# Gram products of an RWKV scan on halves of the rows, and an SSD branch's decay sums from running sums

## The chip, the cores and the metric

The kernel runs on one core of one Trainium2 chip. The metric is the device time of one execution in microseconds (us). A difference of about 0.2% is what a measurement of this kernel can tell from no change.

The core has five engines, each with its own queue of instructions that it works off in order: TensorE (PE, matrix products; its weight loads stand as PEld in the profile), VectorE (DVE), ScalarE (ACT), GpSimd (POOL) and SyncE (SP, which here issues nearly all the DMAs). An instruction that has to wait holds up all that is queued behind it on its engine.

## What is computed

Two networks run one behind the other on 512 tokens of width 1024, with 256 tokens of context. The first is one block of attention beside a state-space branch (SSD), then a feed-forward layer. The second has four layers: a gated spatial unit (SGU), an RWKV-7 scan, a latent attention (MLA) and a second SGU. The change touches the SSD branch and the RWKV scan. What matters of the SSD reference, for chunks of 128 tokens and 32 heads, forward and backward in time:

```python
cs = jnp.cumsum(ac, axis=-1)                       # running sums of the log decays
cb = jnp.einsum('bclgn,bcsgn->bgcls', cc, bc)
scores = cb[:, :, None] * jnp.exp(segsum(ac))      # segsum: cs[l] - cs[s] for s <= l, else -inf
y_diag = jnp.einsum('bgrcls,bcsgrp->bclgrp', scores, xc)
...
yf, hf = ssd_scan(xf, la[:, :, 0], bm, cm, h0f, with_output)
yb, hb = ssd_scan(jnp.flip(xb, axis=1), jnp.flip(la[:, :, 1], axis=1), ...)
y = yf + jnp.flip(yb, axis=1)
```

The RWKV scan carries a 64x64 state per head through the tokens, in both directions, for 16 heads of 64. The kernel works in chunks of 64 tokens. Within a chunk it needs the products of each head's keys with its receptances and removal vectors, masked by time (the Gram products).

## The kernel before

Every large product is made of three products in a rounded format (high by high, high by low, low by high: lines 101 to 103), with weights loaded by SP into the tile `raw` (line 85, two buffers in the SSD stage), split on ACT or DVE into `whi` and on DVE or POOL into `wlo`, three buffers each. Products of plain fp32 tiles stand in the trace as two records each.

A scheduler in the framework sets the order of the instructions on each engine from a simulated timeline. The code's own order, its generators and its `yield`s (one step of filler work for one step of the scan), and the number of buffers of each tile are what it starts from.

**SSD branch** (`ssd`, from about 505 to 1015 us of the trace; the decays, `ssd_steps`, are made earlier, beside the attention). For each of 4 groups of 8 heads `_ssd_scan` goes over 4 chunks, and in each over 2 half groups `hb` of 4 heads: 32 half groups in all. Beside it run as filler the gate products (`pz`) of the same group and the projections (`px`) of the next, and in the last group the attention's output products (`pa`). A half group builds the sums of log decays between every pair of tokens of the chunk as `pE` (128 x 4 heads x 128): for each direction `d` four multiplications of a mask with one column of `laT` (tile `rr`, on ACT for d = 0, line 1903, on DVE for d = 1, line 1901), then one fp32 product with a second mask (line 1904), the two directions summed in PSUM. ACT takes the exponential into `lx` (line 1908). `dm` (ACT, line 1906, then POOL with `cbs`, line 1909) carries the step sizes and the products of B and C. DVE multiplies the two (line 1910), and four products per half group with `xT` give `pyd` (line 1913). `pE` has two buffers and needs nothing of the group's own data, so its products stand well ahead of their use.

**RWKV scan** (`_rwkv_scan`, about 2780 to 3210 us). Two streams `q` of heads go through 12 segments of 4 chunks, the second two steps behind the first; `chunk` is a chain PE, ACT, PE, ACT and DVE, PE, DVE, and the next chunk's first products need its last result. `prepare` readies a stream's next segment one or two steps ahead, with `yield`s between its parts: loads of `kb` and `ar`, four transposes per direction (`pb`), then for each chunk `i` two fp32 Gram products (`d` = 0, 1; line 992) of 128 rows x 256 columns, and a mask product on DVE (`aq`, line 994). 128 rows hold two heads of 64 (`HR[h]`). `ar[:, i, d, h]` is zero in the other head's rows, so one product over all 128 rows gives both heads side by side. `pgm` has two buffers of one PSUM bank each. Other filler in the scan (`late`) is the triangular inverses, on DVE (`_rwkv_diagonal`) and PE (`_rwkv_inverse`).

Of the kernel before, what the change touches and what calls it, by code (L numbers as in the profile page):

```python
# [18 lines left out]
P = 128  # L19
# [917 lines left out]
def _rwkv_scan(K, pools, psum, psp, W, FE, TD, VT, ZD, O, gam, bon, late):  # L937


    nc = K.nc  # L940
    pool = pools[1]
# [4 lines left out]
    HR = ZR  # L946
# [15 lines left out]
    def prepare(n, q, hp, seg, out):  # L962

        st = slice(seg * 4, seg * 4 + 4)
        ar, zv, td, bk = operands(n, q)
        aqs = []
# [22 lines left out]
        for i in range(4):  # L989
            pgm = psp.tile([P, 2, 2, P], F32, tag="pgm", bufs=2, name=K.nm("pgm"))  # L990
            for d in range(2):
                nc.tensor.matmul(pgm[:, d], kb[:, i, d, :], ar[:, i, d], start=True, stop=True)  # L992
            aqs.append(pool.tile([P, 2, 2, P], F32, tag="aq", bufs=10, name=K.nm("aq")))
            nc.vector.tensor_tensor(aqs[i], pgm, mk, op=ALU.mult)
            if i % 2:
                yield
# [668 lines left out]
def ssd_steps(K, XL, XC, W, keep, tmp, S):  # L1665
# [18 lines left out]
    laT = keep.tile([P, 6, 64], F32, name="laT")  # L1684
    ex = keep.tile([P, 6, 192], F32, name="ex")
    wd = keep.tile([P, 6, 64], F32, name="wd")
    S.update(cw=cw, cb=cb, ng=ng, db=db, mk=mk, dtT=dtT, dd=dd, laT=laT, ex=ex, wd=wd)
# [17 lines left out]
    x = laT  # L1705
# [27 lines left out]
    yield  # L1733
    nc.vector.scalar_tensor_tensor(laT, dtT, -1.0, alog.to_broadcast([P, 6, 64]), op0=ALU.mult, op1=ALU.mult)
# [3 lines left out]
    for j in range(6):  # L1738
        d = j % 2
        pe = K.pm.tile([P, 6, 32], F32, tag="m", name=K.nm("pe"))  # L1740
        nc.tensor.matmul(pe, mk[:, j] if j < 4 else K.ones, laT[:, :, d * 32:d * 32 + 32], start=True, stop=True)
        nc.scalar.activation(ex[:, :, j * 32:j * 32 + 32], pe, AF.Exp)
        yield
    nc.vector.tensor_tensor(wd, dtT, ex[:, :, 64:128], op=ALU.mult)
# [93 lines left out]
def _ssd_scan(K, pool, psum, V, g, A, y):  # L1838

    nc = K.nc  # L1840
    dtT, dd, laT, ex, wd, mk = (V[n] for n in ("dtT", "dd", "laT", "ex", "wd", "mk"))
# [36 lines left out]
    for c in range(4):  # L1878
# [12 lines left out]
        for hb in range(2):  # L1891
            h0 = g * 8 + hb * 4
            dm = pool.tile([P, 4, P], F32, tag="dm", bufs=2, name=K.nm("dm"))

            pE = psum.tile([P, 4, P], F32, tag="e", bufs=2, name=K.nm("pE"))
            for d in range(2):
                rr = pool.tile([P, 4, P], F32, tag=f"rr{d}", bufs=1, name=K.nm("rr"))
                for i in range(4):
                    o = d * 32 + h0 + i
                    if d:  # L1900
                        nc.vector.tensor_scalar(rr[:, i, :], mk[:, d], laT[:, t, o:o + 1], None, op0=ALU.mult)
                    else:
                        nc.scalar.activation(rr[:, i, :], mk[:, d], AF.Copy, scale=laT[:, t, o:o + 1])
                nc.tensor.matmul(pE, mk[:, 2 + d], rr, start=d == 0, stop=d == 1)
            for i in range(4):
                nc.scalar.activation(dm[:, i, :], mk[:, 3], AF.Identity, scale=dd[:, t, h0 + i:h0 + i + 1], bias=dtT[:, t, 32 + h0 + i:33 + h0 + i])
            lx = pool.tile([P, 4, P], F32, tag="lx", bufs=2, name=K.nm("lx"))
# [502 lines left out]
```

## Time and profile before

| | us |
|---|---|
| time, median of 3 runs | 4372.11 (4363.34 to 4372.17) |
| the profiled execution's own time | 4365.29 |
| its span, from the first to the last instruction | 4363.5 |
| granted TensorE clock over the span, share of full speed | 0.952 |
| SSD stage, first to last product of the groups' scans | about 505 to 1015 |
| RWKV scan | about 2780 to 3210 |

The page gives the busy time of each engine over the span, the span in 40 slices, the costliest groups of instructions, and the waits. A line of a group or of a timeline names line, engine, operation, the tile written and the tiles read, the shape, and the number of records. A PE record's duration runs until its results have left the array, so records overlap, and the time that a product takes of PE is the distance to the next start. In a timeline equal neighbours are merged: the second number is then the time from the first start to the last end.

### The profile page before, as it was taken

What the parts mean: (1) busy time and instruction counts of PE and PEld (TensorE: products, weight loads), DVE (VectorE), ACT (ScalarE), POOL (GpSimd) and SP (SyncE); (2) the same over time, 40 slices, a digit from 0 to 9 for tenths busy, and PEclk for the clock granted to TensorE, in tenths of its full rate; (3) what the DMA queues carried; (4) which work ended last, traced back from release to release, by engine and by line L of the source; (5) the groups of instructions that cost most, each with busy time, mean ns of one, the idle gap of its engine ahead of it and who ended that gap; (6) DMA issues with size and microseconds to landing.
All of it is one profiled execution on the core that took longest, in us unless ns stands there. A gap on an engine that the chain in (4) does not pass through costs nothing. (4 is left out here: it accounts for less than half of the span.)

```text
span 4363.5 us, 67568 instructions
## 1 busy us (share of the span) xinstructions
PE 4007.8 (92%) x26396; PEld 3288.7 (75%) x26396; DVE 2739.3 (63%) x4361; ACT 1751.1 (40%) x3331; POOL 1507.5 (35%) x1046
## 2 busy tenths in 40 slices
PE   5888999988989999999988989789989999999999
PEld 3766767656766779888977777577777888888987
DVE  6455476676788884445786687865555466663433
ACT  4445445432233334223343555333323465543321
POOL 4333144443444442222344544534411222211221
PEclk7999999988999999999988998899999999999999
DMA  5113121235444553324534667745512311122222
GB/s 190 60 57 99 54 83 51 85 116 169 145 147 150 168 190 117 97 87 139 174 121 158 222 196 225 188 120 143 139 57 92 102 48 51 53 95 92 90 94 87
DMA packets 345550, 518.45 MB, mean 119 GB/s; under 512 B 114424, under 2 KB 217464, under 8 KB 343696
## 3 DMA queue, kind: packets, MB, share of 16 engines
q1 hardware_dynamic: 339040, 502.08, 37.4%
q10 hardware_dynamic: 6192, 12.06, 0.8%
q8 instruction: 208, 3.41, 0.3%
q14 instruction: 110, 0.90, 0.1%
HBM read 425.86 MB, written 88.19 MB: 118 GB/s over the span
## 5 line engine op out<-in xcount | busy, mean ns | idle before, releaser
L93 POOL TENSOR_TENSOR wlo<-raw,whi 128x1024 fp32r<-128x1024 f32 (+2 forms) x254 | 569.6, 2243 | 1332.8 <-ACT whi L91 960.8
L91 ACT ACTIVATE whi<-raw 128x1024 fp32r<-128x1024 f32 (+3 forms) x399 | 383.4, 962 | 706.4 <-PE pz L102 132.2
L95 DVE TENSOR_TENSOR wlo<-raw,whi 128x1024 fp32r<-128x1024 f32 (+3 forms) x278 | 350.2, 1261 | 288.4 <-ACT whi L91 282.1
L127 DVE SCALAR_TENSOR_TENSOR macc<-mraw,conds,macc 128x1024 f32<-128x1024 f32 x168 | 272.0, 1634 | 36.8 <-DMA mraw<-mw 36.5
L103 PE MATMUL pu<-xh,wlo 128*128 128x512 f32 x608 | 243.0, 400 | 10.3 <-DVE wlo L95 6.5
L102 PE MATMUL pu<-xl,whi 128*128 128x512 f32 x608 | 242.1, 398 | 1.1 <-DVE xl L258 1.1
L101 PE MATMUL pu<-xh,whi 128*128 128x512 f32 x608 | 240.4, 399 | 2.9 <-DVE fu L2063 2.4
L89 DVE CAST whi<-raw 128x1024 fp32r<-128x1024 f32 (+2 forms) x133 | 99.5, 748 | 150.1 <-PE pz L102 46.6
L226 POOL TENSOR_TENSOR rsr<-rsv,mhalf 128x4 f32<-128x4 f32 (+3 forms) x56 | 77.9, 1391 | 276.3 <-DVE rsv L224 258.7
L102 PE MATMUL pz<-xl,whi 128*128 128x512 f32 x384 | 150.0, 391 | 0.0
L101 PE MATMUL pv<-whi,xh 128*128 128x256 f32 x512 | 139.0, 283 | 7.0 <-ACT whi L91 6.2
L103 PEld LDWEIGHTS pu<-xh,wlo 128*128 128x128 f32 x608 | 116.0, 191 | 39.0 <-DVE wlo L95 7.3
L102 PE MATMUL pv<-wlo,xh 128*128 128x256 f32 x512 | 142.1, 282 | 0.0
L103 PE MATMUL pv<-whi,xl 128*128 128x256 f32 x512 | 140.2, 282 | 0.5 <-DVE xl L258 0.5
L101 PEld LDWEIGHTS pu<-xh,whi 128*128 128x128 f32 x608 | 116.1, 191 | 31.8 <-issue 3.5
L102 PEld LDWEIGHTS pu<-xl,whi 128*128 128x128 f32 x608 | 116.0, 191 | 29.1 <-DVE xl L258 1.8
L102 PE MATMUL po<-slo,whi 128*128 128x512 f32 (+1 forms) x384 | 136.1, 357 | 0.0
L103 PE MATMUL po<-shi,wlo 128*128 128x512 f32 (+1 forms) x384 | 135.4, 357 | 0.0
L101 PE MATMUL po<-shi,whi 128*128 128x512 f32 (+1 forms) x384 | 133.9, 364 | 0.5 <-ACT shi L111 0.5
L992 PE MATMUL pgm<-ar,kb 128*128 128x256 f32 x384 | 116.8, 427 | 18.9 <-DMA ar<-fe 15.7
L334 POOL TENSOR_TENSOR u<-u,z 128x512 f32<-128x512 f32 (+1 forms) x48 | 58.5, 1218 | 165.2 <-DVE z L325 165.2
L101 PE MATMUL pl<-xlh,whi 128*128 128x512 f32 x208 | 93.3, 452 | 13.2 <-DVE rp L1488 10.2
(747 smaller groups left out, 12923.8 us busy)
## 6 DMA issues: line engine op xcount, KB each, us to landing
mraw<-mw SPq DMA_DIRECT2D x128, 512.0 KB
raw<-G_wuz SPq DMA_DIRECT2D x96, 512.0 KB
raw<-G_wv SPq DMA_DIRECT2D x48, 512.0 KB
raw<-G_wout SPq DMA_DIRECT2D x48, 512.0 KB
raw<-F_w_up SPq DMA_DIRECT2D x44, 512.0 KB
raw<-R_w_in SPq DMA_DIRECT2D x70, 256.0 KB
raw<-S_w_xbc SPq DMA_DIRECT2D x24, 512.0 KB
fe<-ra SPq DMA_DIRECT2D x16, 768.0 KB
```

The source lines that it names most:

```text
L89: nc.vector.tensor_copy(hi, raw)
L91: nc.scalar.activation(hi, raw, AF.Copy)
L93: nc.gpsimd.tensor_tensor(lo, raw, hi.bitcast(F32), op=ALU.subtract)
L95: nc.vector.tensor_tensor(lo, raw, hi.bitcast(F32), op=ALU.subtract)
L101: nc.tensor.matmul(ps, a[0], b[0], start=start, stop=False)
L102: nc.tensor.matmul(ps, a[0], b[1], start=False, stop=False)
L103: return nc.tensor.matmul(ps, a[1], b[0], start=False, stop=stop)
L127: nc.vector.scalar_tensor_tensor(acc, raw, c[:, kt:kt + 1], acc, op0=ALU.mult, op1=ALU.add)
L226: nc.gpsimd.tensor_tensor(r, v, self.mhalf[:, :n], op=ALU.pow)
L334: nc.gpsimd.tensor_tensor(u, u, z, op=ALU.mult)
L992: nc.tensor.matmul(pgm[:, d], kb[:, i, d, :], ar[:, i, d], start=True, stop=True)
```

## The change

There are two parts, and nothing else is edited.

In the RWKV scan a chunk's two Gram products over 128 rows become four over 64 rows: for each direction and head one of `kb[HR[h]]` with `ar[HR[h], ..., h]`, 128 columns wide, so the zero rows are no longer read. `pgm` becomes one tile of two PSUM banks, one bank for each head, holds two chunks, and has one buffer; the mask product of DVE reads it with its dimensions exchanged.

In the SSD branch the running sums of the log decays, of which `ssd_steps` already made the exponentials (`pe`), are also copied as they are (`cum`), transposed, and written to DRAM as rows (`cumrows`, 4 chunks x 64 x 128). In the scan a half group loads for each direction four rows, each spread over all 128 partitions (`cr`, two DMAs of 256 KB on SP's queue, two buffers). ACT adds the negative running sum of the token on the partition to the forward rows, DVE adds it to the backward rows and takes the smaller of the two, the exponential is taken in place, and the product with `dm` too. `rr`, `pE` and `lx` are gone.

```diff
-        for i in range(4):
-            pgm = psp.tile([P, 2, 2, P], F32, tag="pgm", bufs=2, name=K.nm("pgm"))
-            for d in range(2):
-                nc.tensor.matmul(pgm[:, d], kb[:, i, d, :], ar[:, i, d], start=True, stop=True)
...
-            nc.vector.tensor_tensor(aqs[i], pgm, mk, op=ALU.mult)
-            if i % 2:
-                yield
+        for i0 in (0, 2):
+            pgm = psp.tile([P, 2, 2, 2, P], F32, tag="pgm", bufs=1, name=K.nm("pgm"))
+            for i in range(2):
+                for d in range(2):
+                    for h in range(2):
+                        nc.tensor.matmul(pgm[:, h, i, d], kb[HR[h], i0 + i, d, :], ar[HR[h], i0 + i, d, h], start=True, stop=True)
+            for i in range(2):
...
+                nc.vector.tensor_tensor(aqs[i0 + i], pgm[:, :, i].rearrange("p h d t -> p d h t"), mk, op=ALU.mult)
+            yield
...
+        if j < 2:
+            nc.scalar.activation(cum[:, :, j * 32:j * 32 + 32], pe[:, 2:], AF.Copy)
         yield
+        if j == 1:
+            pr = K.pm.tile([64, 4, P], F32, tag="m", name=K.nm("prow"))
+            for t in range(4):
+                nc.tensor.transpose(pr[:, t, :], cum[:, t, :], K.ident)
+            row = raw[:, 0:4 * P].rearrange("h (c t) -> h c t", t=P)
+            nc.scalar.activation(row, pr, AF.Copy)
+            nc.sync.dma_start(rows.rearrange("c h t -> h c t"), row)
+            nc.vector.tensor_scalar(cum, cum, -1.0, None, op0=ALU.mult)
+            yield
...
-            pE = psum.tile([P, 4, P], F32, tag="e", bufs=2, name=K.nm("pE"))
+            cr = pool.tile([P, 2, 4, P], F32, tag="cr", bufs=2, name=K.nm("cr"))
             for d in range(2):
-                rr = pool.tile([P, 4, P], F32, tag=f"rr{d}", bufs=1, name=K.nm("rr"))
-                for i in range(4):
-                    o = d * 32 + h0 + i
-                    if d:
-                        nc.vector.tensor_scalar(rr[:, i, :], mk[:, d], laT[:, t, o:o + 1], None, op0=ALU.mult)
-                    else:
-                        nc.scalar.activation(rr[:, i, :], mk[:, d], AF.Copy, scale=laT[:, t, o:o + 1])
-                nc.tensor.matmul(pE, mk[:, 2 + d], rr, start=d == 0, stop=d == 1)
+                nc.sync.dma_start(cr[:, d], rows[c:c + 1, d, h0:h0 + 4].to_broadcast([P, 4, P]))
+            for i in range(4):
+                nc.scalar.activation(cr[:, 0, i, :], cr[:, 0, i, :], AF.Identity, bias=cum[:, c, h0 + i:h0 + i + 1])
+                nc.vector.scalar_tensor_tensor(cr[:, 0, i, :], cr[:, 1, i, :], cum[:, c, 32 + h0 + i:33 + h0 + i], cr[:, 0, i, :],
+                                               op0=ALU.add, op1=ALU.min)
...
-            nc.scalar.activation(lx, pE, AF.Exp)
+            lx = cr[:, 0]
+            nc.scalar.activation(lx, lx, AF.Exp)
```

The order of the instructions moves with it. On PE in the SSD stage, in the first group's third chunk, before (`pE_5105` is the first half of the fourth chunk, `pyd_4847` the output product):

```order
L103 MATMUL px_5041<-xlh_198,wlo_5002 128x512
L1904 MATMUL pE_5105<-rr_5106,smk 128x512
L1904 MATMUL pE_5105<-rr_5112,smk 128x512
L1870 MATMUL pof_5079<-S_4835,CF_3981 128x512
L1815 MATMUL pxT_4967<-ident,cu_4960 128x128 x4
L1913 MATMUL pyd_4847<-xTl_3977,lx_4866 128x64 x4
L101 MATMUL px_5140<-xch_168,whi_5136 128x256
```

and now, at the same place:

```order
L1832 MATMUL pxT_4927<-ident,cu_4920 128x128 x2
L1888 MATMUL pof_5072<-S_4834,CF_3992 128x512
L1832 MATMUL pxT_4963<-ident,cu_4956 128x128 x4
L1928 MATMUL pyd_4846<-xTl_3988,cr_4848 128x64 x4
L1875 MATMUL pst_5082<-x_1051_5080,BTl_3990 128x512
L1928 MATMUL pyd_4846<-xTl_3988,cr_4970 128x64 x4
L101 MATMUL px_5130<-xch_168,whi_5126 128x256
```

The `pE` products are gone, and the `pyd` products of both half groups stand close together.

On SP in the same stage, before (`raw` are weight loads, `mraw` loads for a later layer's modulation):

```order
L85 DMA raw_5134<-S_w_xbc 128x1024
L85 DMA raw_5240<-S_w_xbc 128x1024
L85 DMA raw_5343<-S_w_xbc 128x1024
L85 DMA raw_5495<-S_w_z 128x1024
L122 DMA mraw_5131<-mw 128x1024
```

and now:

```order
L85 DMA raw_5227<-S_w_xbc 128x1024
L1915 DMA cr_4654<-cumrows 128x512 x2
L1915 DMA cr_4714<-cumrows 128x512 x2
L85 DMA raw_5330<-S_w_xbc 128x1024
L85 DMA raw_5482<-S_w_z 128x1024
L1915 DMA cr_4848<-cumrows 128x512 x2
L1915 DMA cr_4970<-cumrows 128x512 x2
L122 DMA mraw_5121<-mw 128x1024
```

The four `cr` loads of a chunk stand between the weight loads; with two buffers, those of one chunk wait for the `pyd` products of the chunk before.

On PE in the RWKV scan, before (`c` are the chain's products; two different chunks' Gram products, a set of transposes between them):

```order
L1009 MATMUL c_4671_24238<-S_24193,ar_23999 64x64 x2
L992 MATMUL pgm_24410<-ar_24150,kb_24160 128x256 x2
L985 MATMUL pb_24223<-ident,ks_24222 128x128 x4
L992 MATMUL pgm_24415<-ar_24150,kb_24160 128x256 x2
L1014 MATMUL c_4672_24239<-xs_24248,td_24001 64x64
```

and now:

```order
L1012 MATMUL c_4661_24624<-S_24523,ar_23977 64x64 x2
L995 MATMUL pgm_24879<-ar_23914,kb_24490 128x128 x8
L1010 MATMUL c_4674_24688<-zv_24078,aq_24349 64x64 x2
L1012 MATMUL c_4674_24688<-S_24582,ar_24077 64x64 x2
L1010 MATMUL c_4674_24688<-zv_24078,aq_24349 64x64 x2
```

The eight products of two chunks stand in one row here; over the whole scan the Gram products stand in 93 stretches, 98 before.

## Rows read from the trace of the kernel before

**Rows 1.** The page's head: span; busy us (share) and instructions of each engine.
```profile
span 4363.5 us, 67568 instructions
...
PE 4007.8 (92%) x26396; PEld 3288.7 (75%) x26396; DVE 2739.3 (63%) x4361; ACT 1751.1 (40%) x3331; POOL 1507.5 (35%) x1046
```

**Rows 2.** Busy time by stretch: PE, PEld, DVE, ACT, POOL; PEclk; DMA share; GB/s.
```profile
505.00:930.00 425.00, 407.97 (x1933) 303.89 (x1931) 276.46 (x421) 202.22 (x430) 192.32 (x140) 0.97 0.23 72
930.00:1015.00 85.00, 67.99 (x232) 43.48 (x231) 67.96 (x83) 20.37 (x47) 42.10 (x28) 0.86 0.39 130
2800.00:3163.00 363.00, 330.69 (x5456) 266.27 (x5456) 221.82 (x584) 131.86 (x353) 161.76 (x155) 0.96 0.53 139
```

**Rows 3.** PE's timeline, SSD stage: start, us, engine, line, what, records; idle before.
```profile
607.26 1.02 PE L1904 MATMUL pE<-rr,smk 128*128 128x512 f32 x2
608.12 1.02 PE L1870 MATMUL pof<-S,CF 128*128 128x512 f32 x2
...
610.45 1.10 PE L1913 MATMUL pyd<-xTl,lx 128*128 128x64 f32 x8
```

**Rows 4.** Line L1904 over the whole trace: ns min/median/max, first and last start.
```profile
L1904 PE MATMUL pE<-rr,smk x128: 590/592/1191, 467.6 to 956.0; 128*128 128x512 f32 x128
```

**Rows 5.** DVE's groups, 455 to 1015 us: busy, mean ns, idle before by releaser.
```profile
L1901 DVE TENSOR_SCALAR rr<-smk,laT 128x128 f32<-128x128 f32 x128 | 46.8, 425 | 8.5 <-PE pE L1904 5.8 <-DMA ad<-ao 2.5
...
L1910 DVE TENSOR_TENSOR lx<-lx,dm 128x512 f32<-128x512 f32 x32 | 37.0, 1174 | 0.0
```

**Rows 6.** ACT's groups in the same stretch.
```profile
L1906 ACT ACTIVATE dm<-smk,dtT,dd 128x128 f32<-128x128 f32 x128 | 52.2, 483 | 50.3 <-DVE lx L1910 50.3
L1903 ACT ACTIVATE rr<-smk,laT 128x128 f32<-128x128 f32 x128 | 40.7, 390 | 16.0 <-PE pE L1904 15.7
...
L1908 ACT ACTIVATE lx<-pE 128x512 f32<-128x512 f32 x32 | 18.5, 582 | 3.2 <-PE pyd L1913 3.2
```

**Rows 7.** PE's waits, 455 to 985 us: us in total, times, longest.
```profile
PE pyd L1913 <- DVE lx L1910: 5.8, 4, 1.9
```

**Rows 8.** SP's timeline: one weight load's issue.
```profile
675.89 0.33 SPq L85 DMA_DIRECT2D raw<-S_w_xbc  x1
```

**Rows 9.** DVE's timeline: the first work on that load.
```profile
679.12 0.89 DVE L89 CAST whi<-raw 128x1024 fp32r<-128x1024 f32 x1 [1.19 <-PE pz L102]
```

**Rows 10.** SP's own waits, 455 to 985 us.
```profile
SPq L85 <- DVE wlo L95: 258.0, 26, 27.2
```

**Rows 11.** PE's timeline: the pyd products of first chunks of groups 0, 3.
```profile
555.95 1.22 PE L1913 MATMUL pyd<-xTl,lx 128*128 128x64 f32 x10
...
572.63 1.56 PE L1913 MATMUL pyd<-xTl,lx 128*128 128x64 f32 x13
...
928.36 1.00 PE L1913 MATMUL pyd<-xTl,lx 128*128 128x64 f32 x8
...
945.43 1.78 PE L1913 MATMUL pyd<-xTl,lx 128*128 128x64 f32 x15
```

**Rows 12.** PE's timeline in the RWKV scan.
```profile
2937.38 1.13 PE L992 MATMUL pgm<-ar,kb 128*128 128x256 f32 x4
2938.44 0.45 PE L1014 MATMUL c<-xs,td 128*64 128x64 f32 x8
```

**Rows 13.** Lines L992 and L994 over the whole trace.
```profile
L992 PE MATMUL pgm<-ar,kb x384: 379/379/796, 2787.3 to 3161.8; 128*128 128x256 f32 x192
...
L994 DVE TENSOR_TENSOR aq<-pgm,r_rmask x96: 669/684/693, 2790.7 to 3164.8; 128x512 f32<-128x512 f32 x96
```

**Rows 14.** PE's timeline, RWKV features: products on half the rows and columns.
```profile
2420.28 1.61 PE L793 MATMUL pM<-ra,bk 64*64 64x64 f32 x48
```

**Rows 15.** PE's waits in the scan, 2780 to 3210 us.
```profile
PE pgm L992 <- DMA ar<-fe: 15.7, 9, 5.7
```

**Rows 16.** ACT's timeline, the scan's end: the xs copy, the two streams in turn.
```profile
3167.79 0.28 ACT L1011 ACTIVATE xs<-c 128x128 f32<-128x128 f32 x1 [0.63 <-PE c L1009]
...
3171.44 0.28 ACT L1011 ACTIVATE xs<-c 128x128 f32<-128x128 f32 x1 [0.68 <-PE c L1009]
```

More of the change, by code (lines that the diff above doesn't have):

```diff
@@ L987, in prepare @@
         yield
-        for i in range(4):
-            pgm = psp.tile([P, 2, 2, P], F32, tag="pgm", bufs=2, name=K.nm("pgm"))
-            for d in range(2):
-                nc.tensor.matmul(pgm[:, d], kb[:, i, d, :], ar[:, i, d], start=True, stop=True)
-            aqs.append(pool.tile([P, 2, 2, P], F32, tag="aq", bufs=10, name=K.nm("aq")))
-            nc.vector.tensor_tensor(aqs[i], pgm, mk, op=ALU.mult)
-            if i % 2:
-                yield
+        for i0 in (0, 2):
[5 more added lines that the diff above has]
+            for i in range(2):
+                aqs.append(pool.tile([P, 2, 2, P], F32, tag="aq", bufs=10, name=K.nm("aq")))
+                nc.vector.tensor_tensor(aqs[i0 + i], pgm[:, :, i].rearrange("p h d t -> p d h t"), mk, op=ALU.mult)
+            yield
     def chunk(hp, seg, i, tiles, S, y):
@@ L1683, in ssd_steps @@
     dd = keep.tile([P, 6, 32], F32, name="dd")
-    laT = keep.tile([P, 6, 64], F32, name="laT")
     ex = keep.tile([P, 6, 192], F32, name="ex")
     wd = keep.tile([P, 6, 64], F32, name="wd")
-    S.update(cw=cw, cb=cb, ng=ng, db=db, mk=mk, dtT=dtT, dd=dd, laT=laT, ex=ex, wd=wd)
+    x = keep.tile([P, 6, 64], F32, name="cum")
+    cum = x[:, 0:4]
+    rows = K.dram.tile([4, 64, P], F32, name="cumrows")
+    S.update(cw=cw, cb=cb, ng=ng, db=db, mk=mk, dtT=dtT, dd=dd, ex=ex, wd=wd, cum=cum, rows=rows)
     dbias = tmp([P, 1, 64], "dbias")
@@ L1703, in ssd_steps @@
         nc.tensor.transpose(pt[:, t, :], raw[:, t * P:(t + 1) * P], K.ident[0:64, 0:64])
-    x = laT
     nc.vector.tensor_tensor(x, pt, dbias.to_broadcast([P, 6, 64]), op=ALU.add)
@@ L1733, in ssd_steps @@
     yield
+    laT = s
     nc.vector.scalar_tensor_tensor(laT, dtT, -1.0, alog.to_broadcast([P, 6, 64]), op0=ALU.mult, op1=ALU.mult)
@@ L1840, in _ssd_scan @@
     nc = K.nc
-    dtT, dd, laT, ex, wd, mk = (V[n] for n in ("dtT", "dd", "laT", "ex", "wd", "mk"))
+    dtT, dd, ex, wd, mk, cum = (V[n] for n in ("dtT", "dd", "ex", "wd", "mk", "cum"))
+    rows = V["rows"].rearrange("c (d h) t -> c d h t", d=2)
     xT, BT, BF, CF = A["xT"], A["BT"], A["BF"], A["CF"]
@@ L1893, in _ssd_scan @@
             dm = pool.tile([P, 4, P], F32, tag="dm", bufs=2, name=K.nm("dm"))
-            pE = psum.tile([P, 4, P], F32, tag="e", bufs=2, name=K.nm("pE"))
+            cr = pool.tile([P, 2, 4, P], F32, tag="cr", bufs=2, name=K.nm("cr"))
             for d in range(2):
-                rr = pool.tile([P, 4, P], F32, tag=f"rr{d}", bufs=1, name=K.nm("rr"))
-                for i in range(4):
-                    o = d * 32 + h0 + i
-                    if d:
-                        nc.vector.tensor_scalar(rr[:, i, :], mk[:, d], laT[:, t, o:o + 1], None, op0=ALU.mult)
-                    else:
-                        nc.scalar.activation(rr[:, i, :], mk[:, d], AF.Copy, scale=laT[:, t, o:o + 1])
-                nc.tensor.matmul(pE, mk[:, 2 + d], rr, start=d == 0, stop=d == 1)
+                nc.sync.dma_start(cr[:, d], rows[c:c + 1, d, h0:h0 + 4].to_broadcast([P, 4, P]))
[3 more added lines that the diff above has]
+                                               op0=ALU.add, op1=ALU.min)
             for i in range(4):
                 nc.scalar.activation(dm[:, i, :], mk[:, 3], AF.Identity, scale=dd[:, t, h0 + i:h0 + i + 1], bias=dtT[:, t, 32 + h0 + i:33 + h0 + i])
-            lx = pool.tile([P, 4, P], F32, tag="lx", bufs=2, name=K.nm("lx"))
-            nc.scalar.activation(lx, pE, AF.Exp)
+            lx = cr[:, 0]
+            nc.scalar.activation(lx, lx, AF.Exp)
             nc.gpsimd.tensor_tensor(dm, dm, cbs.rearrange("p (o l) -> p o l", o=1).to_broadcast([P, 4, P]), op=ALU.mult)
```

## The prediction, made before the changed kernel ran

> **What bounds the kernel now.** I read the page's head first: PE is busy for 92% of the span and no other engine for more than 63% [rows 1]. What decides is the stage, so the second view was the busy time by stretch [rows 2]. In the SSD stage from 505 to 930 us PE works 408 of 425 us at a granted clock of 0.97, while DVE, ACT and POOL have half their time or more free: PE work taken out there comes off the time nearly whole, until the next engine or a wait takes over. From 930 to 1015 us PE works 68 of 85 us; waits bind there, and work taken from PE is worth less. In the scan PE is busy for 331 of 363 us, but this is many small products of a chain; DVE has 61% and DMA 53%. So the scan is bound mostly by what PE issues, and in part by the chain and by loads.
>
> The third view was PE's timeline, because a record's duration overlaps the next; only distances between starts are PE time.
>
> **SSD: what goes.** A `pE` product (two records) starts at 607.26, the next product at 608.12: 0.86 us, though its line shows 590 ns a record [rows 3, 4]. There are 128 records, hence 64 products: 64 x 0.86 = 55 us of PE. On DVE 128 `rr` (46.8 us) go and 128 additions with a minimum of the same size come, taken at the same 425 ns: even [rows 5]. On ACT 128 `rr` (390 ns) go and 128 additions of a bias come, which are the form of `dm` (483 ns): 128 x 0.09 = +12 us [rows 6]. ACT is 48% busy there [rows 2], so I take this at nothing. If that cover is gone it costs at most these 12 us.
>
> **SSD: what comes.** 64 loads of 256 KB go to SP's queue, and with them a loop that was not there. `pE` needed no load and stood far ahead. Now `cr` has two buffers, one per half group, so the load for a chunk can start only when the `pyd` of the chunk before has read the buffer. One round of that loop: a load of 512 KB takes 3.2 us from issue to first use [rows 8, 9], which is what the two DMAs of a half group move. Then ACT 4 x 0.48 = 1.9, the last DVE addition 0.4, the exponential 0.6, the DVE product 1.2 [rows 5, 6]; for the second half group ACT needs another 1.9 + 0.6; the `pyd` products take 1.0. Sum 10.8 us. Two chunks' `pyd` blocks stand 16.7 and 17.1 us apart in the first and last group [rows 11]. Less four `pE` of 0.86 this becomes 13.3 to 13.7. So the loop fits, with 2.5 to 3 us to spare, when nothing stands in its queues. Something does stand there: ACT and SP work in order. A bias addition that waits for its load holds up the evictions of `pxT`, the convolution's copies and the weight splits behind it, for which PE then waits. And SP's loads stand behind weight loads. Today `pyd` waits only 4 times, 5.8 us in all, for its DVE operand [rows 7]. For the new wait the bounds are 0 (the spare time holds) and 3 us a chunk (the spare time again, used up twice over), times 16 chunks: 0 to 48. I take 1 us a chunk, nearer to rows 7 than to the upper end, because the filler on PE is large products that need no decay: 16 us. SSD together: -55 + 16 = -39, range -55 to -7.
>
> **The decays beside the attention.** Four transposes, three copies, one store and one more step in a stretch of large products: +2 us, 0 to 4, bounded by a few products of 0.1 to 0.4 us and one chain step.
>
> **Scan: what goes and comes.** The 384 Gram records have 256 columns. By `pE` (512 columns in 0.43 us a record) one costs 0.215 us of PE: 83 us. Their stretch of four records took 1.06 us, 0.2 more than that, which is the entry to another tile shape and back [rows 12]; the stretches' number hardly falls (98 to 93 in the order), so that stays. Each record becomes two, on half the rows and with 128 columns. How long is one? 16 `pyd` records (15 are in the row) last 1.78 us: 0.111 each, with 64 columns, where the columns alone would take 0.054 [rows 11]. Loading 128 columns of weights sets that pace, and 128 moving columns also take 0.11. If the two heads' halves run side by side, a pair costs 0.111: 384 x 0.111 = 43 us, a gain of 40. That they do is read from `pM`, whose products on quarters of the array follow at 1.61/48 = 0.03 us [rows 14]; those differ in rows and columns, the new ones in rows only, so the row is near but not the same.
>
> From a product on all rows I would expect 768 x 0.111 = 85 us, no gain. This is where the Trainium skill speaks against the change: "TensorE: Matmul & The Clock Gate", "LDWEIGHTS (loading the stationary operand)", says that a load's time goes by its columns, whatever its rows, and the change doubles the number of loads. By it, with loads in sequence, the sum would be the second rival's below. The same page's "The mechanism" (Part 3) lets work on different row groups overlap; by that the sum is the forecast's. The `pyd` rows agree with the first, `pM` with the second, and no row shows two loads of 128 columns on two halves of the rows.
>
> How much of the 40 reaches the time? The chain is not the bound: a step of one stream, run almost alone at the end, takes 3.65 us [rows 16], while the 96 steps over 363 us (48 for each of two streams) leave 7.6 us for a step of both streams. But PE also waits there, for `ar` loads alone 15.7 us [rows 15], and a shorter scan with 53% DMA [rows 2] will wait more. The mask product on DVE keeps its 669 to 693 ns [rows 13]; one buffer of two banks in place of two of one lets PE fill only when both chunks' masks are done, 1.4 us of DVE, beside other filler. I take 70%: -28, range -45 (all of it and some entries) to -5.
>
> **Sum.** -39 + 2 - 28 = -65. The profiled execution took 4365.3 us (span 4363.5), 6.8 below the median 4372.1: 4300 against its own time, 4307 against the median.
>
> **Rivals.**
>
> *The halves do not overlap* (the change doesn't do what it says). For it: twice the loads, and PEld is at 266 of 363 us already [rows 2]. Against it: `pM`. The scan gives 0: 4372 - 39 + 2 = 4335. Chance 0.12.
>
> *The new loop eats the SSD's gain.* For it: only two buffers, a loop that fits with under 3 us to spare, and an ACT queue in which a load's wait stops unrelated evictions. Against it: PE's filler. It decides at 55/16 = 3.4 us a chunk: 4372 + 2 - 28 = 4346. Chance 0.15.
>
> *Slower than before: `cr` loads stuck on SP.* SP waits in order for a free `raw` buffer: 26 times, 258 us, 9.9 on average, up to 27.2 [rows 10]. A `cr` load behind such a wait arrives that much later, and with two buffers nothing was loaded ahead. Where this hits 12 of 16 chunks in full, it costs 12 x 9.9 = 119: 4372 - 55 + 119 + 2 - 28 = 4410. It turns into a loss from (55 + 28 - 2)/16 = 5 us a chunk. Against it: in the new order a chunk's four loads stand together, one or two weight loads apart from the next, and part of the waiting is spare time before the load is due. Chance 0.08.
>
> *Better than forecast*: the loop costs nothing and the scan gives all its 40: 4372 - 55 + 2 - 40 = 4279. Chance 0.08.
>
> **How the numbers follow.** The forecast, 4285 to 4335 around 4307, has 0.57. The low end 4272 takes in the better case; the high end 4356 takes in the first two rivals with 10 us for their bounds. Left out are the stuck loads and tails of the others, under 0.2. A measurement of this kernel can tell 0.2%, 9 us. Slower by more: 0.09, the third rival with a tail of the second. Same: 0.07, from the second rival with a weak scan. Faster: 0.84.
>
> **What would show it.** The `pE` line is absent and PE in the SSD stage is shorter by about 55 us: step one. PE's wait of `pyd` for the DVE product, 5.8 us before, stays under 20 us, and the waits for `pxT` and split weights don't grow; `pyd` blocks stand 12 to 15 us apart: step two. If they stand at 17 or more, the loop decided, and SP's own waits or ACT's wait for `cr` name which queue. In the scan an eight-product Gram stretch of a chunk pair lasts about 1.1 us if the halves overlap and 2 us if not; the waits for `ar` tell what was given back. The forecast is wrong if these stretches are not shorter per chunk, or if the granted clock, 0.97 and 0.96 in the two stages, falls because PE waits more.

## The result

The changed kernel is slower: 4391.6 us (4380.8 to 4404.3) against 4366.3, ratio 1.0059 with an interval of 1.0046 to 1.0072. I forecast 4307, 65 us under the 4372.1 that stood ahead of the prediction. Its profiled execution took 4384.5 us, 19.2 more than that of before.

The page's head of the changed kernel, then its busy time by stretch (PE, PEld, DVE, ACT, POOL; PEclk; DMA share; GB/s): the SSD stage's two stretches, and the scan from its first Gram product to the first product behind it.

```profile
span 4382.7 us, 68271 instructions
...
PE 3977.6 (91%) x26656; PEld 3301.2 (75%) x26656; DVE 2749.5 (63%) x4362; ACT 1755.1 (40%) x3334; POOL 1522.4 (35%) x1046
...
505.00:930.00 425.00, 382.23 (x1866) 293.80 (x1864) 295.16 (x443) 210.41 (x449) 210.75 (x147) 0.96 0.38 117
930.00:1015.00 85.00, 61.32 (x208) 42.52 (x206) 54.30 (x74) 22.53 (x44) 32.18 (x21) 0.72 0.36 121
...
2777.00:3192.00 415.00, 355.57 (x6159) 302.26 (x6160) 235.45 (x624) 138.96 (x370) 174.25 (x175) 0.85 0.51 128
```

The scan of the kernel before, cut the same way:

```profile
2787.00:3173.00 386.00, 350.97 (x5784) 282.01 (x5784) 238.02 (x624) 138.11 (x372) 175.62 (x177) 0.95 0.54 138
```

PE is busy 30 us less over the span [rows 1], yet the span is longer. The scan takes 415 us in place of 386, at a granted clock of 0.85 in place of 0.95. That is +29, more than the whole loss. The rest is a gain that shrank. Lines with their first and last start show it: the stage's last gate product (`pz`) and the last product of the branch's projection (`py`), before:

```profile
L103 PE MATMUL pz<-xlh,wlo x128: 389/398/799, 519.9 to 931.9; 128*128 128x512 f32 x128
L103 PE MATMUL py<-ox,wlo x128: 387/389/795, 1057.7 to 1155.7; 128*128 128x512 f32 x128
```

and after:

```profile
L103 PE MATMUL pz<-xlh,wlo x128: 389/399/799, 512.9 to 906.6; 128*128 128x512 f32 x128
L103 PE MATMUL py<-ox,wlo x128: 388/389/793, 1039.3 to 1145.0; 128*128 128x512 f32 x128
```

25 us were gained at the last gate product, and 11 are left 240 us later, about as many as when the scan begins (2776.9, before 2787.3). So the profiled execution is 10 us ahead at the start of the scan and loses 29 in it: +19. These are two single executions; the medians differ by 25 us.

**The halves do overlap.** PE's timeline of the changed kernel, two stretches of eight Gram products (two chunks) and what follows each:

```profile
3001.89 2.08 PE L995 MATMUL pgm<-ar,kb 64*128 64x128 f32 x16
3003.90 0.69 PE L1022 MATMUL c<-zv,bk 128*64 128x64 f32 x8
...
3007.42 1.16 PE L995 MATMUL pgm<-ar,kb 64*128 64x128 f32 x16
3008.51 0.66 PE L1130 MATMUL pt<-ident,y 128*128 128x128 f32 x4
```

and their line over the whole trace (ns min/median/max, first and last start):

```profile
L995 PE MATMUL pgm<-ar,kb x768: 272/272/579, 2776.9 to 3181.2; 64*128 64x128 f32 x192
```

Sixteen records in 1.16 us, of 0.27 us each, start (1.16 - 0.27)/15 = 0.06 us apart, 0.12 a pair where I had 0.111. The stretch takes 1.09 us to the next start, where two chunks took 2 x 1.06 [rows 12]. That is the 1.1 us that the prediction named as the sign of overlap: two heads at once, and two loads of 128 columns did not follow one another. "The mechanism" (Part 3) of the Trainium skill's "TensorE: Matmul & The Clock Gate" lets loads overlap work on other row groups. The trace agrees with it. (Loads in sequence would have given the prediction's first rival, 4335, and not "the second rival's" sum, as is written there.) The earlier stretch, the same work, takes 2.01 us: its granted clock was 0.50, 1.2 GHz.

### The profile page after: what moved, and what is told of

The parts are those of the page before. It is cut to its first block, busy times and chain, and to the rows that moved or that the text cites. A ratio compares the mean times of both kernels' runs of the same rounds, so it can differ in the third digit from the quotient of the medians.

```text
span 4382.7 us, 68271 instructions
## 1 busy us (share of the span) xinstructions
PE 3977.6 (91%) x26656; PEld 3301.2 (75%) x26656; DVE 2749.5 (63%) x4362; ACT 1755.1 (40%) x3334; POOL 1522.4 (35%) x1046
## 5 line engine op out<-in xcount | busy, mean ns | idle before, releaser
L127 DVE SCALAR_TENSOR_TENSOR macc<-mraw,conds,macc 128x1024 f32<-128x1024 f32 x168 | 258.1, 1552 | 21.2 <-DMA mraw<-mw 20.5
L995 PE MATMUL pgm<-ar,kb 64*128 64x128 f32 x768 | 91.2, 334 | 24.3 <-DMA ar<-fe 12.1
L887 DVE TENSOR_TENSOR tm<-lm,lw 128x31 f32<-128x31 f32 (+15 forms) x186 | 93.1, 501 | 19.6 <-DMA lm<-md 13.5
```

Of the source, the lines that this page charges most:

```text
L127: nc.vector.scalar_tensor_tensor(acc, raw, c[:, kt:kt + 1], acc, op0=ALU.mult, op1=ALU.add)
L887: nc.vector.tensor_tensor(tv, lm[:, 0:u, u:u + 1].to_broadcast([P, u, 32 - u]), lw[:, u:u + 1, u:32].to_broadcast([P, u, 32 - u]), op=ALU. ...
L995: nc.tensor.matmul(pgm[:, h, i, d], kb[HR[h], i0 + i, d, :], ar[HR[h], i0 + i, d, h], start=True, stop=True)
```

## Experiments

Times are medians beside runs of the kernel before on the same chip (its median was 4365 to 4370 in each of these groups, so a comparison across groups can be off by some us). "Scan" is always cut as above.

### The two parts apart, and what PE's time in the scan is worth

`gram_only` and `ssd_only` take one part each. `gram_one_head` saves the same 40 us of PE without halves, by leaving out the other head's products:

```diff
-                nc.tensor.matmul(pgm[:, d], kb[:, i, d, :], ar[:, i, d], start=True, stop=True)
+                nc.tensor.matmul(pgm[:, d, 0], kb[:, i, d, :], ar[:, i, d, 0], start=True, stop=True)
```

`pairs_full_rows` has the new tile and steps with the old products:

```diff
-                    for h in range(2):
-                        nc.tensor.matmul(pgm[:, h, i, d], kb[HR[h], i0 + i, d, :], ar[HR[h], i0 + i, d, h], start=True, stop=True)
+                    nc.tensor.matmul(pgm[:, i, d], kb[:, i0 + i, d, :], ar[:, i0 + i, d], start=True, stop=True)
...
```

> The Gram part alone, the SSD branch as before. In the trace of the changed kernel the scan, from its first Gram product to the first product behind it, took 415.3 us in place of 385.8 (+29.5). Theory order (the chain now waits behind filler in PE's queue): the loss belongs to this part, time of before +25 to +32, PE's waits for zv and ks as in the changed kernel. Theory clock (half-row products let the granted clock fall): the same total, and a mean clock in the scan near 0.85. If the loss came from the SSD part in some way, this one would be 20 to 40 us faster than before.

> The SSD part alone, the scan as before. In the changed kernel the last gate product of the SSD stage ended 25.4 us sooner, but by the end of the branch's output projection only 10.7 us were left. Expected: 8 to 14 us faster than before, the scan with its old duration (385 us). If the give-back behind the SSD stage belonged to the changed scan, 25 us faster.

> The kernel before, but each Gram product reads the columns of one head alone (128 in place of 256), over all rows, and the mask product reads that half twice: the other head's products are left out. Buffers, yields and their places as before; PE loses 384 x 0.1 = 40 us of issue, as much as side-by-side halves were to save. Theory order: the scan is not bound by what PE issues, gain 0 to 10 us. Theory clock, with PE's issue as the bound: gain 25 to 35 us, the clock as before, near 0.95.

> The Gram part's tile and steps (two chunks per pgm, one buffer of two banks, one yield behind both) with the old products over all 128 rows and 256 columns. Theory order: the pairs in one buffer do the harm, 15 to 40 us slower than before. Theory clock: within 6 us of before, the clock in the scan near 0.95.

Measured: `gram_only` 4404.7 (1.0090, 1.0064 to 1.0116), `ssd_only` 4378.9 (1.0031, 1.0020 to 1.0043), `gram_one_head` 4339.4 (0.9939, 0.9918 to 0.9961), `pairs_full_rows` 4376.5 (1.0025, 1.0011 to 1.0038). Their scans, in this order:

```profile
2783.00:3209.00 426.00, 358.76 (x6153) 304.93 (x6155) 234.16 (x626) 139.28 (x370) 173.03 (x177) 0.83 0.50 126
```

```profile
2789.00:3185.00 396.00, 355.25 (x5784) 289.68 (x5783) 232.47 (x615) 138.70 (x372) 171.23 (x169) 0.92 0.51 132
```

```profile
2782.00:3148.00 366.00, 315.16 (x5810) 274.82 (x5811) 239.59 (x628) 138.35 (x373) 177.25 (x179) 0.92 0.58 146
```

```profile
2786.00:3187.00 401.00, 352.19 (x5797) 290.94 (x5798) 234.75 (x623) 138.86 (x372) 174.28 (x175) 0.92 0.53 132
```

`gram_one_head` gains 27 us for 40 us of PE: some 70% reach the time, as I had assumed, and the theory that the scan isn't bound by PE falls; but its clock is 0.92 and not the expected 0.95, and its trace has 20 us of the gain in the scan. The Gram part as halves loses 38 us, more than the 25 to 32 that I expected. The pairs alone cost 10 of them, between the two theories, so the halves make some 28 us worse what should be 40 less. And `ssd_only` loses 12 us where I expected a gain of 8 to 14: its scan, in which nothing is edited, takes 396 us. The two parts' losses, 38 and 12, don't add up to the changed kernel's 25: each kernel has an order of its own.

### Half of the rows, and the clock

`one_head_64rows` is `gram_one_head` on the 64 rows that are not zero. `halves_and_full` adds 96 products over all rows ahead of the halves, 83 us more for PE. `four_full_rows` is `gram_only` with every half product over all 128 rows, so PE has 42 us more to issue. `halves_single` has halves, one chunk at a time:

```diff
-                nc.tensor.matmul(pgm[:, d, 0], kb[:, i, d, :], ar[:, i, d, 0], start=True, stop=True)
+                nc.tensor.matmul(pgm[:, d, 0], kb[HR[0], i, d, :], ar[HR[0], i, d, 0], start=True, stop=True)
...
+            for h in range(2):
+                nc.tensor.matmul(pgm[:, h].rearrange("p i d t -> p (i d) t"), kb[:, i0, 0, :], ar[:, i0:i0 + 2, :, 0], start=True, stop=True)
...
-                        nc.tensor.matmul(pgm[:, h, i, d], kb[HR[h], i0 + i, d, :], ar[HR[h], i0 + i, d, h], start=True, stop=True)
+                        nc.tensor.matmul(pgm[:, h, i, d], kb[:, i0 + i, d, :], ar[:, i0 + i, d, h], start=True, stop=True)
```

> One head's Gram products alone, as in the run with 128 of 256 columns (4339 us), but on that head's 64 rows: the zero rows are no longer read, the products, their number, columns, buffers and steps are the same; the other head's products are left out in both. Theory clock (PE working on half its rows lets the granted clock fall): clock in the scan near 0.85 in place of 0.92, 20 to 40 us slower than 4339, 4360 to 4380. Theory order (the halves are well, but the pairs of chunks and the order they bring are not): the same time within 8 us, clock near 0.92.

> The Gram part alone, and ahead of each pair of chunks two more products over all 128 rows and 512 columns into the same tile, overwritten by the halves: 96 products, 192 records of 0.43 us = 83 us more for PE. Theory clock: the added work keeps the clock up (over 0.9 in the scan, 0.83 without), and pays for more than half of itself: under 40 us slower than the Gram part alone (4405). Theory order: 60 to 85 us slower than it, 4465 to 4490, the clock unchanged.

> The Gram part alone, with its pairs of chunks, its tile and its four products of 128 columns per chunk, but each over all 128 rows (the zero rows are read again): PE has the Gram products' old cost of 85 us and not 43. Theory clock: the clock in the scan is back above 0.9, and although PE has 42 us more to issue, the time is no longer than with the halves (4405) and near that of the pairs with 256 columns: 4370 to 4390. Theory order: the halves did save their 40 us and the pairs' order costs more, so this is 30 to 45 us slower than the halves, 4435 to 4450.

> Halves of the rows, but one chunk at a time and the yields as before (a tile of two banks, half filled, one buffer). If the pairs in one buffer are what costs (10 us with full rows), this is 10 us faster than the Gram part alone, 4390 to 4397. If the halves themselves cost by the clock, it stays 25 us or more over the kernel before, with a clock in the scan under 0.88.

Measured: 4361.1 (0.9997, 0.9980 to 1.0015), 4450.7 (1.0197, 1.0182 to 1.0213), 4389.6 (1.0046, 1.0028 to 1.0064) and 4402.8 (1.0083, 1.0059 to 1.0108). Their scans:

```profile
2789.00:3168.00 379.00, 337.18 (x5809) 287.54 (x5809) 238.51 (x628) 138.55 (x373) 178.01 (x179) 0.88 0.56 141
```

```profile
2788.00:3257.00 469.00, 418.16 (x6379) 306.80 (x6381) 236.05 (x622) 138.26 (x372) 172.37 (x175) 0.94 0.44 113
```

```profile
2785.00:3198.00 413.00, 362.54 (x6160) 322.14 (x6159) 232.98 (x625) 139.63 (x370) 173.96 (x177) 0.92 0.51 129
```

```profile
2781.00:3209.00 428.00, 363.61 (x6189) 307.29 (x6191) 239.17 (x626) 138.79 (x373) 174.17 (x178) 0.83 0.49 125
```

The same products with the zero rows left out cost 22 us (4361 against 4339), the clock falls from 0.92 to 0.88. Reading the zero rows again, with 42 us more for PE, makes the Gram part 15 us faster (4390 against 4405), the clock is at 0.92 in place of 0.83. The 83 us of added full products cost 46, the clock is at 0.94; I had set the line at 40, so this one alone would decide nothing. Taking the chunks singly changes nothing (4403, 0.83), so the pairs are not the main harm. Expected clocks were met in all but `one_head_64rows` (0.88 for 0.85). Four kernels whose Gram products are halves alone (the changed one among them), in different orders, stand at 0.83 to 0.88. The fifteen kernels here whose Gram products are all over full rows, most of them with an order of their own, stand at 0.91 to 0.95.

What a low clock costs here is seen in `gram_only` in stretches at one level or the other, the chain's products `c` alone (PE busy and records; PEclk; DMA share; GB/s):

```profile
2936.80:2950.40 13.60, 6.69 (x173) 1.00 0.77 159
2950.40:2964.10 13.70, 6.94 (x105) 0.50 0.26 62
2964.10:3005.10 41.00, 20.50 (x517) 1.00 0.51 130
3005.10:3025.60 20.50, 7.59 (x104) 0.50 0.71 147
3025.60:3046.00 20.40, 9.09 (x226) 1.00 0.39 110
3046.00:3063.10 17.10, 7.45 (x105) 0.50 0.44 101
3063.10:3090.40 27.30, 13.88 (x337) 1.00 0.54 124
```

At 2.4 GHz 1253 records in 102.3 us, 12.2 each us; at 1.2 GHz 314 in 51.3 us, 6.1. The scan runs at half pace there, waits included. What PE did as the clock fell at 3005, from PE's timeline:

```profile
3002.98 0.43 PE L1017 MATMUL c<-xs,td 128*64 128x64 f32 x8
3006.82 1.12 PE L985 MATMUL pb<-ident,ks 128*128 128x128 f32 x4 [3.41 <-POOL ks L983]
```

It stood in front of a transpose whose operand POOL had not finished, with the chain's products queued behind it. This is one fall of twelve in that scan.

If time at 1.2 GHz is worth half, clock times length is the scan's length at 2.4 GHz throughout, an estimate from the rows above, of one execution each: 367 for the kernel before (0.95 x 386), 354 for `gram_only`, 353 for the changed kernel, 355 for `halves_single`, 380 for `four_full_rows`, 337 for `gram_one_head` and 334 for `one_head_64rows`. So the halves do save 13 us at full clock (26 against the same steps on full rows), and the half pace takes 62 to 73 us in place of 19. The last two kernels, 22 us apart in time, are equal by this measure.

### Where the SSD part's gain goes

`ssd_one_load` loads the rows once a group into a constant tile. `ssd_act_queue` issues the loads from ACT, and `ssd_split` also puts the two directions into tiles of their own. `pe_one_direction` is the kernel before without the second `pE` product, so its sums lack one direction:

```diff
-                nc.sync.dma_start(cr[:, d], rows[c:c + 1, d, h0:h0 + 4].to_broadcast([P, 4, P]))
+                nc.scalar.dma_start(cr[:, d], rows[c:c + 1, d, h0:h0 + 4].to_broadcast([P, 4, P]))
...
-            cr = pool.tile([P, 2, 4, P], F32, tag="cr", bufs=2, name=K.nm("cr"))
+            cf = pool.tile([P, 4, P], F32, tag="cf", bufs=3, name=K.nm("cf"))
+            cb = pool.tile([P, 4, P], F32, tag="cb", bufs=2, name=K.nm("cb"))
...
-                nc.tensor.matmul(pE, mk[:, 2 + d], rr, start=d == 0, stop=d == 1)
+                if d == 0:
+                    nc.tensor.matmul(pE, mk[:, 2 + d], rr, start=True, stop=True)
```

> The SSD part alone, but the rows are loaded once for each group and not for each half group, so the sums are wrong for all but the first half group (the exponential takes a thousandth of them); all operations of ACT, DVE, POOL and PE stay, and the result goes to a tile of its own with two buffers. The scan's order on PE is the same as in the run of the SSD part. Theory loop (loads and their two buffers eat the gain): the last gate product of the SSD stage comes 10 to 20 us sooner than in the SSD part alone, and the time is 4360 to 4370 in place of 4379. Theory DVE (slower operations and another order, not the loads): within 5 us of 4379. The scan, which has the same order, should have the length of the SSD part's, 396 us.

> The SSD part alone, its 64 row loads issued by ACT and not by SP. If the wait behind weight loads on SP is the loop's price: the SSD stage 10 us shorter. If the loop is slow by its own steps: no change in the stage. The scan's order on PE is closer to that of the kernel before (0.94 of its rows in common, 0.67 for the SSD part); if the order is what made the scan 11 us longer with the SSD part, it is 386 to 390 us here.

> The SSD part alone with its loads on ACT's queue and with the two directions in tiles of their own: forward rows in three buffers, backward rows in two, which come free as soon as DVE has read them and not only after the pyd products. Theory loop: the last gate product comes 3 to 6 us sooner than with the shared tile on ACT's queue (909.5), near the 903.7 us of the run that loads once, and the time is 4355 to 4362. If the buffers were not the limit: as that run, 4367.

> The kernel before without the second direction's pE products (32 of 64 left out, 27.5 us of PE; the tile rr for them is still made). Theory that PE's work in this stage comes off the time whole and the new loop ate the SSD part's gain: the last gate product comes 20 to 27 us sooner. Theory that the stage is bound by other engines once PE has less to do: under 15 us.

Measured: 4362.1 (0.9995, 0.9981 to 1.0008), 4367.3 (1.0005, 0.9992 to 1.0018), 4363.7 (0.9990, 0.9979 to 1.0001) and 4366.5 (0.9997, 0.9981 to 1.0013). The last `pz` and `py` products of `ssd_only`, then of `ssd_one_load`, `ssd_act_queue`, `ssd_split` and `pe_one_direction`:

```profile
L103 PE MATMUL pz<-xlh,wlo x128: 389/396/799, 516.0 to 911.2; 128*128 128x512 f32 x128
L103 PE MATMUL py<-ox,wlo x128: 387/389/795, 1046.0 to 1151.1; 128*128 128x512 f32 x128
```

```profile
L103 PE MATMUL pz<-xlh,wlo x128: 387/396/799, 514.3 to 903.7; 128*128 128x512 f32 x128
L103 PE MATMUL py<-ox,wlo x128: 387/389/796, 1033.8 to 1139.4; 128*128 128x512 f32 x128
```

```profile
L103 PE MATMUL pz<-xlh,wlo x128: 388/396/799, 513.1 to 909.5; 128*128 128x512 f32 x128
L103 PE MATMUL py<-ox,wlo x128: 387/389/794, 1037.6 to 1138.1; 128*128 128x512 f32 x128
```

```profile
L103 PE MATMUL pz<-xlh,wlo x128: 389/396/799, 513.5 to 904.4; 128*128 128x512 f32 x128
L103 PE MATMUL py<-ox,wlo x128: 387/389/796, 1033.8 to 1135.0; 128*128 128x512 f32 x128
```

```profile
L103 PE MATMUL pz<-xlh,wlo x128: 388/396/799, 525.6 to 914.4; 128*128 128x512 f32 x128
L103 PE MATMUL py<-ox,wlo x128: 388/389/737, 1034.8 to 1135.8; 128*128 128x512 f32 x128
```

How far single executions can be trusted here is seen from `ssd_split` and three kernels told below that differ from it in the scan alone: their last `pz` stands at 904.4 to 910.7, their last `py` at 1135.0 to 1138.8. The loads cost 8 us by the last gate product, hardly more than that spread, and 12 by the last `py`; another queue and split tiles win all of that back. What the split tiles add to ACT's queue, 5 and 3 us, is within the spread, and the time (4363.7) is 2 us above the range I gave it. Even without the loads only 28 of the 55 us of PE come off by the last `pz`, while leaving out 27.5 us of `pE` brings 18 there, between my two theories, and 20 by the last `py`: in this stage some two thirds of PE's time come off. ACT's queue alone wins 13 us by the last `py`, so SP's queue is most of the loads' price; in the stage itself it wins 2 us and not the 10 that I had written. So the stage's gain with a repaired loop is 17 to 28 us. But none of these times falls by 20 us, though the scan is not touched in any of them.

### Why an untouched scan grows

The scheduler makes another order of the scan for each of these kernels. Three swaps of two equal steps in the kernel before tell what an order is worth: the directions of `pE` (in the SSD stage), the directions of the Gram products, and the loads of `ar` ahead of those of `kb`:

```diff
-            for d in range(2):
+            for d in (1, 0):
                 rr = pool.tile([P, 4, P], F32, tag=f"rr{d}", bufs=1, name=K.nm("rr"))
...
-            for d in range(2):
+            for d in (1, 0):
                 nc.tensor.matmul(pgm[:, d], kb[:, i, d, :], ar[:, i, d], start=True, stop=True)
...
-            nc.sync.dma_start(kb[:, :, d, :], FE[hp][d][1][:, st])
             for h in range(2):
                 nc.sync.dma_start(ar[HR[h], :, d, h, :], FE[hp][d][0][HR[h], st])
+            nc.sync.dma_start(kb[:, :, d, :], FE[hp][d][1][:, st])
```

> The kernel before with the two directions of pE taken in the other order: no work added or removed, nothing in the scan edited, but the scan's order on PE has only 0.70 of its rows in common with before. Theory order: the scan takes 392 to 410 us and the time is 8 to 20 us longer. Theory early start: the stage ends when it did, the scan takes 386 +- 5 us.

> The kernel before with the two Gram products of a chunk in the other order: the same work, 0.39 of the scan's rows on PE in common with before. Theory order: scan 392 to 410 us, time 8 to 20 us longer. Theory early start: 386 +- 5 us.

> The kernel before with the loads of ar ahead of those of kb in a segment's preparation: the same work, 0.70 of the scan's rows on PE in common with before. Theory order: scan 392 to 410 us. Theory early start: 386 +- 5 us, or a little less, since PE waits for ar loads.

Measured: 4385.0 (1.0040, 1.0026 to 1.0054), 4378.3 (1.0020, 1.0008 to 1.0032) and 4383.5 (1.0033, 1.0018 to 1.0048), beside 4370.3 for the kernel before. Their scans:

```profile
2795.00:3198.00 403.00, 359.52 (x5786) 292.09 (x5787) 231.22 (x612) 139.56 (x372) 172.62 (x170) 0.92 0.51 130
```

```profile
2787.00:3181.00 394.00, 345.64 (x5783) 284.17 (x5783) 239.78 (x619) 139.17 (x371) 174.93 (x172) 0.95 0.52 133
```

```profile
2787.00:3195.00 408.00, 359.66 (x5785) 291.65 (x5786) 236.14 (x625) 139.43 (x372) 175.31 (x177) 0.92 0.51 131
```

All three are slower by 8 to 15 us with the same work. Two begin their scans when the kernel before does; `swap_pe` begins 8 us later, so a part of its loss lies ahead of the scan. The kernel before has a good order in its scan. Eleven other kernels with its full Gram products and other orders (the three swaps and the eight runs of the SSD stage, the three told next among them) took 392 to 409 us for the scan, it 386. A length is one execution's, though: `ssd_one_load`, with `ssd_only`'s order of PE in the scan, took 407 us where I expected its 396, and `ssd_split` and `pe_one_direction`, with one order, 400 and 409. So the swaps' medians carry the verdict, not the lengths. The repaired SSD runs lose most of some 20 us after a stage that ends that much sooner; the swaps would explain 8 to 15 of it. Whether an early start costs the rest is open.

The repaired SSD part was then run with three such swaps in the scan:

> The SSD part with loads on ACT's queue and split tiles (4364 us, its scan 399 us), and the loads of ar ahead of those of kb in the scan. Theory order: the SSD stage's 21 us stay, and the scan takes whatever this order brings, 385 to 410 us: 4345 to 4375. Theory early start: the scan again 395 to 410 us, whatever the order.

> The repaired SSD part, with the two Gram products of a chunk in the other order (0.38 of the scan's PE rows in common with before). Theory order: SSD stage 20 us sooner as in the other repaired runs, the scan anywhere from 385 to 410 us: 4345 to 4375, most likely 4360.

> The repaired SSD part, with the two directions' transposes in the other order (0.55 of the scan's PE rows in common with before). Theory order: the same range, 4345 to 4375.

Measured: 4364.3 (0.9991, 0.9978 to 1.0005), 4362.2 (0.9996, 0.9981 to 1.0011) and 4374.5 (1.0019, 1.0006 to 1.0032). Their scans take 395, 392 and 407 us. All times are in the range, and none beats the kernel before clearly. The scans fit the theory of the order; 392 is too close to the other theory's 395 to rule it out. The best, `ssd_split`, ends at 0.9990 with an interval that reaches 1.0001.

## Why the prediction was wrong, point by point

**Scan, what reaches the time: wrong in sign.** The halves cost 0.12 us a pair in long stretches, near the 0.111 worked out, and 70% is what 40 us of PE bring in the median when half of the products are left out on full rows (`gram_one_head`: 27). The step that failed is the clock: the term of -28 prices the scan at the clock of the kernel before, and the sentence on the clock stands at the very end as a condition, with no price and no chance. In place of -28 the scan took 29 us more, at a clock of 0.85 in place of 0.95.

That sentence's reason, "because PE waits more", holds in part. In the changed kernel's scan PE is idle for 59 us (415 less 355.6 busy), before for 35. One of its waits, before and after:

```profile
PE c L1019 <- DVE zv L1016: 4.3, 3, 2.9
```

```profile
PE c L1022 <- DVE zv L1019: 13.8, 11, 5.0
```

But waits alone don't set the clock. `gram_one_head` leaves PE idle for 51 of 366 us, as large a share as in the changed kernel, and was granted 0.92. `one_head_64rows`, whose four records of a chunk take as long to the next start (0.64 us at 2901.43, against 0.65 at 2905.20 in `gram_one_head`), idles for 42 of 379 us and was granted 0.88. In it the clock stood at 1.2 GHz for 20.5 us in which PE was never idle, and after 6.8 us at 2.4 GHz, again without idle time, it fell once more:

```profile
2912.70:2933.20 20.50, 20.50 (x247) 17.86 (x249) 7.72 (x22) 7.35 (x19) 10.16 (x10) 0.50 0.56 119
2933.20:2940.00 6.80, 6.80 (x152) 6.05 (x148) 3.16 (x10) 2.23 (x8) 0.00 (x0) 1.00 0.46 136
2940.00:2943.40 3.40, 3.40 (x52) 3.06 (x52) 1.21 (x5) 0.36 (x2) 0.00 (x0) 0.50 0.00 0
```

What differs most is how long the clock stays low. The four scans with halves alone have 9 to 17 stretches at 1.2 GHz, of 8.5 to 11 us on average; the fifteen with full rows have 7 to 14, of 4.6 to 6.6 us. Why half-filled rows keep the clock low for longer, no run shows.

That the clock can differ was in the rows: it was 0.97 and 0.86 in the two stretches of the SSD stage [rows 2]. It should have been a rival: a scan at 0.85 in place of 0.95 loses 0.10 x 386 = 39 us, all of the gain.

**SSD, what goes: right in PE's time, too large in what it brings.** The term of -39 came out as -25 by the last gate product and as -10 by the start of the scan. 505 to 930 us lost 26 us of PE's busy time at nearly the same clock (382.2 against 408.0 [rows 2]). 408 of 425 us busy did not mean that PE's time comes off "nearly whole": `pe_one_direction` brought two thirds.

**SSD, the loop: the right wait, the wrong place.** The groups of DVE and ACT in the changed kernel's SSD stage (busy, mean ns of one, idle before by releaser):

```profile
L1918 DVE SCALAR_TENSOR_TENSOR cr<-cr,cum 128x128 f32<-128x128 f32 x128 | 58.6, 513 | 14.3 <-ACT cr L1917 7.3 <-DMA cr<-cumrows 6.4 <-ACT cbs L1901 0.5
L1917 ACT ACTIVATE cr<-cr,cum 128x128 f32<-128x128 f32 x128 | 41.2, 391 | 41.8 <-DMA cr<-cumrows 39.4 <-PE pcb L1899 1.2 <-PE px L103 1.2
```

ACT stood 39 us for the loads. The additions on DVE took 513 ns in place of 425: 12 us where I wrote "even"; on ACT 391 and not 483, even where I wrote +12. PE's own wait for `pyd` rose only from 5.8 [rows 7] to 8.4 us, under the 20 that I had named as the sign of success. But the `pyd` blocks of the chunks came no closer. In PE's timeline, the first and the last block of the last group, after, then in `ssd_one_load`, and the last block before (its first starts at 928.36 [rows 11]):

```profile
902.98 1.00 PE L1928 MATMUL pyd<-xTl,cr 128*128 128x64 f32 x8
...
955.51 1.60 PE L1928 MATMUL pyd<-xTl,cr 128*128 128x64 f32 x8
```

```profile
900.16 1.00 PE L1925 MATMUL pyd<-xTl,lx 128*128 128x64 f32 x8
...
952.61 1.08 PE L1925 MATMUL pyd<-xTl,lx 128*128 128x64 f32 x8 [0.19 <-DVE lx L1922]
```

```profile
980.79 3.52 PE L1913 MATMUL pyd<-xTl,lx 128*128 128x64 f32 x16
```

That is 52.5 us for three steps, 17.5 a step, where before it was 52.4: by the prediction's sign, "17 or more", "the loop decided". But `ssd_one_load`, which has no load in the loop, also takes 52.4, so the sign doesn't single out the loads, and what spaces the blocks is not shown. The 16.7 and 17.1 that the prediction started from are first steps alone; before, the steps within a group run from 14 to 26 us. So the "2.5 to 3 us to spare" was read from too few rows.

SP's own waits show where the loads stood, after:

```profile
SPq L1915 <- DVE cr L1925: 43.3, 8, 13.5
...
SPq L1915 <- PE pyd L1928: 24.8, 14, 5.0
```

The `cr` loads waited for their buffers, and held up what stood behind them on SP. That this has a price is shown by `ssd_act_queue` (13 us by the last `py`), not by these rows. From the last gate product to the last `py` the gain fell from 25 to 11 us. The third rival saw SP as the place but turned it round, with `cr` behind weights.

**What was left out altogether.** That an edit moves the order of a scan that it doesn't touch; three neutral swaps cost 8 to 15 us of the time. `ssd_only` had 5 us left by the last `py`, none as its scan began, and lost 11 in the scan. Of the changed kernel's own 29 us I can't say how much is order and how much is clock, since `one_head_64rows` and `four_full_rows`, too, differ from their partners in order. That halves bring a lower clock rests on four kernels against fifteen, whose ranges (0.83 to 0.88, 0.91 to 0.95) don't meet, and not on one pair.

## What to carry to other kernels

Where a chain of small products runs among filler, TensorE time that is saved is worth its price only while the granted clock holds: price the scan at the lower clock too, as a rival of its own. A test kernel that leaves out as much work on full rows tells what the saving is worth by itself (here it gained 27 us, while the halves lost 38). Before a small gain is believed or given up, swap two equal steps elsewhere and see what a mere reordering does; here it was 8 to 15 us, beside the 25 that the whole change lost. A load that replaces computed data needs a queue on which nothing urgent stands behind its wait for a buffer.

## What the runs showed of the hardware

Products on two halves of the rows start 0.06 us apart, two at a time, with loads of 128 columns each. The scan with half-row Gram products was granted a clock of 0.83 to 0.88 (four kernels), with full rows 0.91 to 0.95 (fifteen). Adding 83 us of TensorE work to it raised the clock from 0.83 to 0.94 and cost 46 us. A run's time goes with its mean clock: the ten of `pe_one_direction` go from 4351.3 us at 0.951 to 4381.6 at 0.942. In most other kernels the link is looser, and which of the two causes the other is not shown. Four runs each of `halves_and_full` and `four_full_rows` agree to within 3 us (4449.8 to 4451.8 and 4389.0 to 4391.6), though their clocks go from 0.949 to 0.952 and from 0.947 to 0.951.
